# A two-layer decoder: gate weights stationary and tokens moving, a new order around the compressed blocks, transposes of layer 0 behind two more steps, and another split of the last output tile

## The chip, the cores and the metric

The kernel runs on one core of a Trainium2 chip. Its engines work side by side, each through its own queue in order: TensorE (PE in the profile; PEld is its loading of weights), VectorE (DVE), ScalarE (ACT), GpSimd (POOL) and SyncE (SP), which here issues transfers. The metric is the device time of one execution in microseconds (us), the median of several runs. Lower is better.

## The reference

The input is 256 tokens of 1024 numbers. Everything is float32.

```
h  = x + stick_breaking_attention(rms_norm(x)) @ w_o          # 16 heads of 64
h  = h + squared_relu_mlp(rms_norm(h))                         # 1024 -> 4096 -> 1024
kv = rms_norm(h) @ w_kv                                        # shared: compressed, selected, window
     hid = gelu(blocks of 32 tokens, stride 16, + cmp_pos) @ cmp_w1)
     k_cmp, v_cmp = hid @ cmp_w2                               # 15 compressed blocks, 4 groups
q, gate logits = rms_norm(h) @ w_q
gates = sigmoid(gate logits + gate_b)                          # 3 for each of 16 heads
h  = h + (gates * [compressed, selected, window attention]) @ w_o
h  = h + squared_relu_mlp(rms_norm(h))
out = rms_norm(h)
```

Stick-breaking attention takes its weights from a running sum over the keys of log(1 - sigmoid(z)), and so needs, for each pair of heads, Exp, Ln, a scan, a subtraction and one more Exp between the scores z and the product with the values.

## The kernel before, in words

Tokens lie in two tiles of 128 (`t`). A product is made of three matmuls: every float32 operand is split into a rounded part and the rest (`wh` by a cast on ACT, line 125; `wl` by a subtraction on DVE, line 126), and L177, L178 and L179 (`mm3`) multiply high by high, high by low, low by high. L182 (`mm`) is a single matmul, L185 (`tr`) a transpose on PE. Weights come in one stream of transfers on SP into three raw slots, and are split into three slots of `wh` and `wl`; `step()` splits the next half as the program goes on.

*Layer 0.* `proj(n)` makes queries and keys of head pair n with 48 matmuls of 256 columns, six for each of eight k. `inside(n)` inserts the attention of earlier pairs ahead of k = 5 (k = 2 for n = 1): `scores(n-1)` (8 matmuls into z, then the chain of Exp, Ln, scan L507, subtraction L508 and Exp L509), `turn(n-2)` (six transposes, L519, into pa, then copies) and `values(n-3)` (8 matmuls, po). The last pairs are inserted into the out projection at places (i, n, kk).

*Layer 1.* The table `NSA` at the head of the file is the order of its pieces by name. PE is held to that order. A scheduler of the language places the instructions of the other engines, whose queues then run in order. The names that matter here: `kv` projections of keys and values, `gt` and `ga` the transposes and gathers of compressed blocks, `gp` the gates, `cw` the first product of the compressed blocks, `ge` their gelu (copy, Square, Exp, Ln, Exp on ACT, products on DVE), `ch` the transposes of the hidden values (pht), `ck` compressed keys and values (pkc, pvc), `q` a group's half of the query projection (24 matmuls), `qr` its rotation, `S` the scores of a head pair (8 matmuls into z), `M` their softmax weights, `T` the transposes of these (ptp), `V` the values, `o` the out projection. Letters such as 'zzaz' choose between two sets of four PSUM banks, `bank` ('a') and `bank2` ('z'). The function that makes the gates holds the tokens as the stationary operand and moves 96 (high part) or 48 (low part) gate columns: 8 k, two token tiles, two matmuls each.

*The end.* The second MLP accumulates into four banks. Its last products go tile by tile, the last of them in two pieces of 256 columns (`by_t`; the second piece into a bank of its own, accq). `finish` adds each piece to the residual (L268), takes the sum of squares (ACT, L963), the product with the norm's weight (DVE), at the last piece the power on POOL, and scales the tile: ACT columns 0 to 511, DVE 512 to 1023, each followed by a transfer of 256 KB out, on ACT's and on SP's queue.

Of the kernel before, what the change touches and what calls it, by code (L numbers as in the profile page):

```python
# [14 lines left out]
P = 128  # L15
# [21 lines left out]

NSA = (
# [16 lines left out]
def hybrid_kernel(ctx, tc, x, xcols, eye, gcols, gfin, wqk, wv, wo0, wkv, wq, wg, rot, wo1, w1, w2, cw1, cw2, cpos, gate_b, consts, out):  # L55
# [19 lines left out]
    def bank(name, dt=F32):  # L75
        return ps.tile([P, 512], dt, tag="a", name=name, bufs=4)

    def bank2(name):
        return ps.tile([P, 512], F32, tag="z", name=name, bufs=4)
# [101 lines left out]
    def mm(o, a, b, first, last):  # L181
        pe(nc.tensor.matmul(o, a, b, start=first, stop=last, skip_group_check=True))  # L182
# [12 lines left out]
    def tok(xt, k, t):  # L195
        return xt[0][:, k, t * P:(t + 1) * P], xt[1][:, k, t * P:(t + 1) * P]
# [92 lines left out]
    def mlp(layer, gi, xt, mid, ap):  # L289

        wa, wb = i_m[layer]
        acc = [[None, None], [None, None]]
        held = []
        r2 = []

        def second(items, order, hook=None):
            for i, (t, n, q) in enumerate(order):
                if hook is None and i % 2 == 0:
                    step()
                for c, hT, w in items:  # L300
                    for f in range(2):
                        if c == 0 and f == 0:
                            acc[n][t] = bank(f"acc{t}{n}")
                        if q.start and c == items[0][0] and f == 0:

                            acc[n][t] = bank2("accq")
                        o = f * D + n * 512
                        mm3(acc[n][t][:, q], tok(hT, f, t), cut(w, o + q.start, o + q.stop),
                            f == 0 and c == (items[0][0] if q.start else 0), c == NFC - 1 and f == 1)
                if hook is not None:  # L310
                    hook(i, t, n, q)

        whole = slice(0, 512)
        by_n = [(t, n, whole) for n in range(2) for t in range(T)]

        by_t = [(t, n, whole) for t in range(T) for n in range(2)][:-1] + [(1, 1, slice(0, 256)), (1, 1, slice(256, 512))]

        begun = {}

        def begin(c):  # L320

            w = W(wa[c])
            begun[c] = w, [bank2(f"pu{f}") for f in range(2)]
            if c < 2:
                products(c, [(f, k, i) for k in range(NK // 2) for f in range(2) for i in range(2)])

        def products(c, ks, done=None):
            w, pu = begun[c]
            for j, (f, k, i) in enumerate(ks):
                if j % 16 == 0 and (c or j):  # L330
                    step()
                wide(pu[f], cut(w, k * 256 + f * P, k * 256 + (f + 1) * P), xt, k, i, k == 0, k == NK - 1)
                if k == NK - 1 and i:
                    done(f, pu[f])

        def first(c):
            if c not in begun:
                begin(c)
            r = ap.tile([P, 512], F32, name="mr")
            u = ap.tile([P, 512], F32, name="mu")  # L340
            s = ap.tile([P, 512], F32, name="ms")

            def done(f, pu):

                q = slice(f * 256, (f + 1) * 256)
                nc.scalar.copy(r[:, q], pu[:, 256:512])  # L346
                nc.vector.tensor_add(u[:, q], pu[:, 0:256], r[:, q])  # L347

            products(c, [(f, k, i) for f in range(2) for i in range(2) for k in range(NK // 2 if c < 2 else 0, NK)], done)
            nc.vector.scalar_tensor_tensor(s, u, 0.0, u, op0=OP.max, op1=OP.mult)  # L350
            hh = ap.tile([P, 2, T * P], F32R, name="hh", bufs=3)
            hl = ap.tile([P, 2, T * P], F32R, name="hl", bufs=3)
            sv = s.rearrange("p (f q) -> p f q", f=2)
            nc.scalar.copy(hh, sv)  # L354
            nc.vector.tensor_sub(hl, sv, f32(hh))  # L355
            return hh, hl


        begin(0)
        pt = xt_tr(1, bank)  # L360
        begin(1)
        xt_evac(pt, 1, gi, xt)
        for c in range(NFC):
            hT = first(c)
            if c == 0:
                for t in range(T):
                    r = sp.tile([P, 1], F32, name="r2", bufs=4)
                    nc.vector.reciprocal(r, var_of([hres[t]]))
                    r2.append(r)
            if 0 < c < NFC - 1:  # L370
                second([held.pop(0) + (W(wb[c - 1]),)], by_n)
            held.append((c, hT))

        def hook(i, t, n, q):
            res(n, t, acc[n][t], r2[t], q if q.start else whole)
            mid(i, t, n, q)

        second([it + (W(wb[it[0]]),) for it in held], by_t if layer else by_n, hook)

    def layer0(ap):  # L380
# [152 lines left out]


        def inside(n):
            return {2 if n == 1 else 5: [lambda f=f, p=n - d: f(p) for d, f in ((1, scores), (2, turn), (3, values)) if n >= d]}

        for n in range(NP):
            proj(n, inside(n))
        xn = xt_tiles("n")  # L540
        out_proj(oT, i_o0, {(0, 0, 2): [lambda: scores(NP - 1), lambda: values(NP - 3)],
                            (0, 1, 0): [lambda: turn(NP - 2)], (0, 1, 2): [lambda: values(NP - 2)],
                            (1, 0, 0): [lambda: turn(NP - 1)], (1, 0, 1): [lambda: values(NP - 1)],
                            (1, 1, 2): [lambda: xt_evac(xt_tr(0), 0, 1, xn)]})
        return xn
# [1 line left out]
    def nsa(xk, pt0, ap):  # L547
# [63 lines left out]
        M = NG * NC  # L611
        blk = [None, None]
        ph = None

        def gather_tr(c):
            live["g", c] = []
# [52 lines left out]
        gates = ap.tile([P, T, 48], F32, name="gates")  # L669

        def gate_proj():
            pg = bank("pg")
            for k in range(NK):
                for t in range(T):
                    h, lo = tok(xq, k, t)
                    mm(pg[:, t * 96:(t + 1) * 96], h, wgp[:, k].rearrange("p a c -> p (a c)"), k == 0 and t == 0, False)
                    mm(pg[:, t * 96:t * 96 + 48], lo, wgp[:, k, 0, :], False, k == NK - 1)
            g2 = ap.tile([P, T, 96], F32, name="g2", tag="pe", bufs=6)
            for t in range(T):
                nc.scalar.activation(g2[:, t], pg[:, t * 96:(t + 1) * 96], AF.Copy, scale=rstd[t])  # L680
            nc.vector.tensor_add(gates, g2[:, :, 0:48], g2[:, :, 48:96])
            nc.vector.tensor_add(gates, gates, gbs[:, None, :].to_broadcast([P, T, 48]))
            nc.vector.tensor_scalar(gates, gates, -80.0, None, op0=OP.max)
            nc.scalar.activation(gates, gates, AF.Exp, scale=-1.0)
            nc.vector.tensor_scalar(gates, gates, 1.0, None, op0=OP.add)
            nc.vector.reciprocal(gates, gates)

            nc.vector.tensor_tensor(gates[:, :, 0:NH], gates[:, :, 0:NH],
                                    cst[:, C_ANY:C_ANY + T][:, :, None].to_broadcast([P, T, NH]), op=OP.mult)

        live = {}

        qu = big([P, NG, 2, T * P], F32, "qu")
        qr = big([P, NG, 2, T * P], F32, "qr")
# [228 lines left out]
        def tokens_n():  # L923
# [3 lines left out]


        strict[0] = True
        do = {"kv": kv_proj, "xq": tokens_q, "rt": rot_tables, "gt": gather_tr, "ga": gather, "gp": gate_proj, "kr": keys_rope,  # L930
              "cw": cw_proj, "kt": keys_tr, "q": q_proj, "qr": q_rot, "ge": gelu, "ch": cmp_hid, "ck": cmp_kv, "S": scores,
              "M": weights, "T": turn, "V": values, "cp": cmp_probs, "ct": cmp_tr, "o": o_proj, "r": residual, "xn": tokens_n,
              "w": step}
# [25 lines left out]
    def finish(i, t, n, q):  # L959
# [12 lines left out]
            return  # L972
        r = sp.tile([P, 1], F32, name="r", bufs=4)
        nc.gpsimd.tensor_tensor(r, v, npow, op=OP.pow)
        nc.scalar.activation(y[:, 0:512], y[:, 0:512], AF.Copy, scale=r)
        nc.vector.tensor_scalar(y[:, 512:1024], y[:, 512:1024], r, None, op0=OP.mult)
        nc.scalar.dma_start(out[t * P:(t + 1) * P, 0:512], y[:, 0:512])
        nc.sync.dma_start(out[t * P:(t + 1) * P, 512:1024], y[:, 512:1024])

    scoped(mlp, "m1", 1, 3, xn, finish)  # L980

# [93 lines left out]
```

## Time and profile before

| | us |
|---|---|
| median of the runs | 630.44 (629.31, 630.44, 630.53) |
| the profiled execution | 631.12 |
| its span, first to last instruction | 629.3 |
| mean granted TensorE clock | 0.995 |
| PE busy | 617.7 (98%) |
| DVE busy | 418.1 (66%) |
| ACT busy | 344.5 (55%) |

A row of the timeline gives start, length, engine, line, operation, output <- inputs, and in brackets the idle time ahead of it and what ended that. A row of the waits gives the total, the count and the longest. A row of the chain of waits gives start, length to the next step of the chain, engine, tile and line. Matmuls overlap their neighbours, so their spacing is less than their length.

### The profile page before, as it was taken

The numbers are of one execution on the slowest core, as the hardware profiler recorded it, in microseconds if no ns is written. First come the engines' busy times: TensorE is split into PE (matmuls) and PEld (weight loads), VectorE is DVE, ScalarE is ACT, GpSimd is POOL, SyncE is SP. The second block draws the span as 40 slices with busy tenths as digits, with TensorE's granted clock in tenths as the row PEclk, the third lists the DMA queues.
The fourth block names the chain that finished last, engine by engine and source line by source line (L and its number), as shares of the span: only waits on it lengthen the run. The fifth ranks groups of instructions, "written<-read, shape, count | busy, mean of one in ns | idle before, by whom it ended". The sixth has DMA issues, their size and how long they took to land.

```text
span 629.3 us, 9078 instructions
## 1 busy us (share of the span) xinstructions
PE 617.7 (98%) x3569; PEld 518.4 (82%) x3569; DVE 418.1 (66%) x667; ACT 344.5 (55%) x592; POOL 55.4 (9%) x76
## 2 busy tenths in 40 slices
PE   8999999999999999999999989999999999999996
PEld 5899987888888888888888867777888888888885
DVE  5587887766566666656783599863685656666555
ACT  5666666465444445443852597773565544444533
POOL 0100000000000000000322164460000000000000
PEclk9999999999999999999989999999999999999999
DMA  8863333446555455553554731303455554545501
GB/s 290 348 262 135 134 134 117 159 168 227 200 169 203 169 206 191 201 200 135 175 212 189 276 125 70 101 2 134 134 200 202 193 201 154 205 184 200 202 0 68
DMA packets 17755, 108.12 MB, mean 172 GB/s; under 512 B 2352, under 2 KB 3248, under 8 KB 5680
## 3 DMA queue, kind: packets, MB, share of 16 engines
q1 hardware_dynamic: 16416, 105.84, 46.5%
q10 hardware_dynamic: 1296, 1.70, 0.9%
q8 instruction: 28, 0.46, 0.3%
q14 instruction: 15, 0.12, 0.1%
HBM read 106.48 MB, written 1.05 MB: 171 GB/s over the span
## 4 chain that ended last, share of the span: by engine, by line
PE 91%; DVE 3%; ACT 3%; issue 1%; DMA 1%; SPq 0%; POOLq 0%; POOL 0%; DVEq 0%
PE pu L182 28%; PE acc L177 12%; PE acc L178 11%; PE acc L179 11%; PE po L182 3%; PE qk L177 2%; PE qk L179 2%; PE qk L178 2%; PE z L182 2%; PE pk L177 2%; PE pk L179 2%; PE pk L178 2%; PE ptp L185 1%; ACT pe L850 1%; PE ph L182 1%; PE pv L177 1%
## 5 line engine op out<-in xcount | busy, mean ns | idle before, releaser
L126 DVE TENSOR_TENSOR wl<-raw,wh 128x1024 fp32r<-128x1024 f32 (+1 forms) x190 | 226.6, 1228 | 126.3 <-ACT wh L125 125.2
L125 ACT CAST wh<-raw 128x1024 fp32r<-128x1024 f32 (+1 forms) x190 | 189.5, 1041 | 105.4 <-PE acc L179 50.7
L182 PE MATMUL pu<-xn,wh 128*128 128x512 f32 x512 | 132.1, 392 | 0.0
L182 PEld LDWEIGHTS pu<-xn,wh 128*128 128x128 f32 x512 | 93.7, 188 | 18.0
L177 PE MATMUL acc<-wh,hh 128*128 128x512 f32 (+1 forms) x256 | 99.9, 390 | 0.0
L178 PE MATMUL acc<-wl,hh 128*128 128x512 f32 (+1 forms) x256 | 99.7, 389 | 0.0
L179 PE MATMUL acc<-wh,hl 128*128 128x512 f32 (+1 forms) x256 | 98.8, 388 | 0.0
L182 PE MATMUL pu<-xn,wl 128*128 128x256 f32 x512 | 76.5, 282 | 0.0
L182 PEld LDWEIGHTS pu<-xn,wl 128*128 128x128 f32 x512 | 72.1, 190 | 5.1
L179 PEld LDWEIGHTS acc<-wh,hl 128*128 128x128 f32 x256 | 48.1, 188 | 10.7 <-DVE hl L355 0.6
L177 PEld LDWEIGHTS acc<-wh,hh 128*128 128x128 f32 x256 | 48.2, 188 | 10.1 <-ACT hh L354 0.9
L178 PEld LDWEIGHTS acc<-wl,hh 128*128 128x128 f32 x256 | 48.2, 188 | 8.7
L354 ACT CAST hh<-ms 128x512 fp32r<-128x512 f32 x32 | 19.8, 620 | 63.1 <-DVE ms L350 63.1
L346 ACT COPY mr<-pu 128x256 f32<-128x256 f32 x64 | 23.6, 368 | 28.3 <-PE pu L182 28.3
L177 PE MATMUL qk<-xa,wh 128*128 128x256 f32 x128 | 36.9, 288 | 0.0
L179 PE MATMUL qk<-xa,wl 128*128 128x256 f32 x128 | 36.3, 283 | 0.0
L178 PE MATMUL qk<-xa,wh 128*128 128x256 f32 x128 | 36.2, 283 | 0.0
L355 DVE TENSOR_TENSOR hl<-ms,hh 128x512 fp32r<-128x512 f32 x32 | 22.1, 691 | 19.2 <-ACT hh L354 19.2
L864 POOL TENSOR_TENSOR pe<-pe,rs 128x512 f32<-128x512 f32 (+1 forms) x32 | 32.3, 1038 | 25.4 <-DVE rs L859 10.0
L850 ACT ACTIVATE pe<-pe,nm 128x256 f32<-128x256 f32 (+1 forms) x64 | 28.2, 443 | 6.3 <-DVE nm L848 4.6
L347 DVE TENSOR_TENSOR mu<-pu,mr 128x256 f32<-128x256 f32 x64 | 26.6, 418 | 7.5 <-ACT mr L346 7.5
L177 PE MATMUL acc<-wh,oT 128*128 128x512 f32 x64 | 26.3, 411 | 0.0
(184 smaller groups left out, 860.1 us busy)
## 6 DMA issues: line engine op xcount, KB each, us to landing
raw<-in_w SPq DMA_DIRECT2D x64, 1024.0 KB, 4.8
raw<-in_wqk SPq DMA_DIRECT2D x8, 1024.0 KB, 5.0
raw<-in_wo SPq DMA_DIRECT2D x8, 1024.0 KB, 4.8
raw<-in_wkv SPq DMA_DIRECT2D x6, 1024.0 KB, 4.8
raw<-in_wq SPq DMA_DIRECT2D x4, 1024.0 KB, 4.8
wc<-in_cw SPq DMA_DIRECT2D x4, 1024.0 KB, 7.6
raw<-in_wv SPq DMA_DIRECT2D x7, 512.0 KB, 8.5
hres<-in_x SPq DMA_DIRECT2D x2, 512.0 KB, 8.8
```

What stands on the lines that cost most here:

```text
L125: nc.scalar.copy(h[:, r], raws[j][:, r])
L126: nc.vector.tensor_sub(lo[:, r], raws[j][:, r], f32(h[:, r]))
L177: pe(nc.tensor.matmul(o, a[0], b[0], start=first, stop=False, skip_group_check=True))
L178: pe(nc.tensor.matmul(o, a[0], b[1], start=False, stop=False, skip_group_check=True))
L179: pe(nc.tensor.matmul(o, a[1], b[0], start=False, stop=last, skip_group_check=True))
L182: pe(nc.tensor.matmul(o, a, b, start=first, stop=last, skip_group_check=True))
L346: nc.scalar.copy(r[:, q], pu[:, 256:512])
L347: nc.vector.tensor_add(u[:, q], pu[:, 0:256], r[:, q])
L354: nc.scalar.copy(hh, sv)
L355: nc.vector.tensor_sub(hl, sv, f32(hh))
L850: nc.scalar.activation(e, e, AF.Exp, scale=-1.0, bias=nm[:, hd, t, b:b + 1], accum_out=rs[:, hd, t, b:b + 1])
L864: nc.gpsimd.tensor_tensor(sv, sv, rs[:, hd, t, :][:, :, None].to_broadcast([P, 2, n]), op=OP.mult)
```

## The change

Five things change. `turn(n-2)` leaves the common insertion and goes ahead of k = 7; in the out projection three insertions become one at (0, 0, 3). The gates hold the weights (96 or 48 columns) and move all 256 tokens, so 16 matmuls make the transposed gates; ACT copies them out, and a new piece `gq` behind `gt` 1 transposes them back with two transposes, before the same elementwise work. In the table, `q` 1 0 goes behind `cw` 1, `ge` ahead of `q` 1 1, and `ch` and `ck` go ahead of `q` 2 0 and `q` 2 1. The last output tile is cut at 384 of 512 columns instead of 256. In the final scaling ACT has 384 columns and DVE 640, and the transfers are cut there too.

```diff
 NSA = (
-    ('ga', 0), ('gp',), ('kv', 2, 0), ('gt', 1), ('kr', 0), ('kv', 2, 1), ...
-    ... ('qr', 0), ('q', 1, 0), ('kt', 1),
-    ('cw', 1, 0), ('cw', 1, 1), ('q', 1, 1), ('S', 0, 'zzaz'), ('M', 0), ('ge',), ('qr', 1), ('S', 1, 'azzz'), ('M', 1), ('q', 2, 0),
-    ('q', 2, 1), ('ch',), ('w',), ('T', 0, 'zaa'), ('S', 2, 'azaz'), ('ck',), ('q', 3, 0), ('T', 1), ('qr', 2),
+    ('ga', 0), ('gp',), ('kv', 2, 0), ('gt', 1), ('gq',), ('kr', 0), ('kv', 2, 1), ...
+    ... ('qr', 0), ('kt', 1),
+    ('cw', 1, 0), ('cw', 1, 1), ('q', 1, 0), ('ge',), ('q', 1, 1), ('S', 0, 'zzaz'), ('M', 0), ('qr', 1), ('ch',),
+    ('q', 2, 0), ('S', 1), ('M', 1), ('ck',), ('q', 2, 1), ('w',), ('T', 0, 'zaa'), ('S', 2, 'azaz'), ('q', 3, 0),
+    ('T', 1), ('qr', 2), ...
...
-        by_t = [(t, n, whole) for t in range(T) for n in range(2)][:-1] + [(1, 1, slice(0, 256)), (1, 1, slice(256, 512))]
+        by_t = [(t, n, whole) for t in range(T) for n in range(2)][:-1] + [(1, 1, slice(0, 384)), (1, 1, slice(384, 512))]
...
         def inside(n):
-            return {2 if n == 1 else 5: [lambda f=f, p=n - d: f(p) for d, f in ((1, scores), (2, turn), (3, values)) if n >= d]}
+            h = {2 if n == 1 else 5: [lambda f=f, p=n - d: f(p) for d, f in ((1, scores), (3, values)) if n >= d]}
+            if n >= 2:
+                h[7] = [lambda: turn(n - 2)]
+            return h
...
-        out_proj(oT, i_o0, {(0, 0, 2): [lambda: scores(NP - 1), lambda: values(NP - 3)],
-                            (0, 1, 0): [lambda: turn(NP - 2)], (0, 1, 2): [lambda: values(NP - 2)],
+        out_proj(oT, i_o0, {(0, 0, 3): [lambda: scores(NP - 1), lambda: values(NP - 3), lambda: turn(NP - 2)],
+                            (0, 1, 2): [lambda: values(NP - 2)],
...
         def gate_proj():
-            pg = bank("pg")
+            pg = bank2("pg")
             for k in range(NK):
-                for t in range(T):
-                    h, lo = tok(xq, k, t)
-                    mm(pg[:, t * 96:(t + 1) * 96], h, wgp[:, k].rearrange("p a c -> p (a c)"), k == 0 and t == 0, False)
-                    mm(pg[:, t * 96:t * 96 + 48], lo, wgp[:, k, 0, :], False, k == NK - 1)
+                mm(pg[0:96, 0:T * P], wgp[:, k].rearrange("p a c -> p (a c)"), xq[0][:, k, :], k == 0, False)
+                mm(pg[0:48, 0:T * P], wgp[:, k, 0, :], xq[1][:, k, :], False, k == NK - 1)
+            gT = ap.tile([96, T * P], F32, name="gT", tag="pe", bufs=6)
+            nc.scalar.copy(gT, pg[0:96, 0:T * P])
+            live["gT"] = gT
+
+        def gate_turn():
+            pg = bank2("pgt")
+            gT = live.pop("gT")
+            for t in range(T):
+                pe(nc.tensor.transpose(pg[:, t * 96:(t + 1) * 96], gT[:, t * P:(t + 1) * P], ident[0:96, 0:96]))
             g2 = ap.tile([P, T, 96], F32, name="g2", tag="pe", bufs=6)
...
-        nc.scalar.activation(y[:, 0:512], y[:, 0:512], AF.Copy, scale=r)
-        nc.vector.tensor_scalar(y[:, 512:1024], y[:, 512:1024], r, None, op0=OP.mult)
-        nc.scalar.dma_start(out[t * P:(t + 1) * P, 0:512], y[:, 0:512])
-        nc.sync.dma_start(out[t * P:(t + 1) * P, 512:1024], y[:, 512:1024])
+        m = 384
+        nc.scalar.activation(y[:, 0:m], y[:, 0:m], AF.Copy, scale=r)
+        nc.vector.tensor_scalar(y[:, m:D], y[:, m:D], r, None, op0=OP.mult)
+        nc.scalar.dma_start(out[t * P:(t + 1) * P, 0:m], y[:, 0:m])
+        nc.sync.dma_start(out[t * P:(t + 1) * P, m:D], y[:, m:D])
```

On PE, in layer 0, this is one of the insertions inside the projections as the two programs differ (rows of the change with +, of before with -):

```order
 L182 MATMUL z_573<-qkT 128x128
 L182 MATMUL z_574<-qkT 128x128
-L519 MATMUL pa<-ident,sbe 128x128 x6
 L182 MATMUL po<-sbt,v_92 64x256 x2
 L182 MATMUL po<-sbt,v_92 64x128 x2
```
```order
 L178 MATMUL qk<-xa,wh 128x256
 L179 MATMUL qk<-xa,wl 128x256
+L519 MATMUL pa<-ident,sbe 128x128 x6
 L177 MATMUL qk<-xa,wh 128x256
 L178 MATMUL qk<-xa,wh 128x256
```

The six transposes stood between scores and values; they now stand alone among projection matmuls, 12 of these later.

On ACT, around the gelu of layer 1 (hx and hu are its tiles, qu the queries of a group, pe the softmax weights, hidT the turned hidden values), before:

```order
L740 COPY hx<-ph 60x512
L125 CAST wh<-raw 128x1024
L712 ACTIVATE qu<-pq 128x512
L743 ACTIVATE hu<-hx 60x512
L850 ACTIVATE pe,rs<-pe,nm 128x256 x4
L850 ACTIVATE pe,rs<-pe,nm 128x128 x4
L125 CAST wh<-raw 128x1024
L746 ACTIVATE hu<-hu 60x512
L850 ACTIVATE pe,rs<-pe,nm 128x256
L747 ACTIVATE hu<-hu 60x512
L850 ACTIVATE pe,rs<-pe,nm 128x256
L748 ACTIVATE hu<-hu 60x512
```

and in the change:

```order
L749 COPY hx<-ph 60x512
L752 ACTIVATE hu<-hx 60x512
L755 ACTIVATE hu<-hu 60x512
L756 ACTIVATE hu<-hu 60x512
L125 CAST wh<-raw 128x1024
L757 ACTIVATE hu<-hu 60x512
L721 ACTIVATE qu<-pq 128x512
L859 ACTIVATE pe,rs<-pe,nm 128x256 x4
L859 ACTIVATE pe,rs<-pe,nm 128x128 x4
L767 COPY hidT<-pht 128x240
```

The gelu no longer stands among the softmax weights of two head pairs; its last Exp stands behind one weight cast.

On DVE, at the very end (v is the mean of squares so far), before:

```order
L964 TENSOR_TENSOR ys_4138<-hres_72,gf 128x256
L969 SCALAR_TENSOR_TENSOR v<-ssq_4136 128x1
L268 SCALAR_TENSOR_TENSOR hres_72<-accq,r_4235,hres_72 128x256
L971 COPY ssq_4136<-v 128x1
L964 TENSOR_TENSOR ys_4138<-hres_72,gf 128x256
```

and in the change:

```order
L973 TENSOR_TENSOR ys_4127<-hres_72,gf 128x384
L978 SCALAR_TENSOR_TENSOR v<-ssq_4125 128x1
L980 COPY ssq_4125<-v 128x1
L268 SCALAR_TENSOR_TENSOR hres_72<-accq,r_4224,hres_72 128x128
L973 TENSOR_TENSOR ys_4127<-hres_72,gf 128x128
```

The copy of v stands ahead of the last addition where it stood behind it, and the last pieces are half as wide.

More of the change, by code (lines that the diff above doesn't have):

```diff
@@ L613, in nsa @@
         ph = None
+        live = {}
         def gather_tr(c):
@@ L689, in gate_proj @@
                                     cst[:, C_ANY:C_ANY + T][:, :, None].to_broadcast([P, T, NH]), op=OP.mult)
-        live = {}
         qu = big([P, NG, 2, T * P], F32, "qu")
@@ L929, in nsa @@
         strict[0] = True
-        do = {"kv": kv_proj, "xq": tokens_q, "rt": rot_tables, "gt": gather_tr, "ga": gather, "gp": gate_proj, "kr": keys_rope,
+        do = {"kv": kv_proj, "xq": tokens_q, "rt": rot_tables, "gt": gather_tr, "ga": gather, "gp": gate_proj, "gq": gate_turn, "kr": keys_rope,
               "cw": cw_proj, "kt": keys_tr, "q": q_proj, "qr": q_rot, "ge": gelu, "ch": cmp_hid, "ck": cmp_kv, "S": scores,
```

6 rows, old and new, of the table NSA are left out of this document.

## The prediction

> **What bounds the kernel now.** I read the page's totals first, then the waits of TensorE (PE), the chain of waits, and the timeline and windows at the places that the change touches. The totals of the page:
>
> ```profile
> PE 617.7 (98%) x3569; PEld 518.4 (82%) x3569; DVE 418.1 (66%) x667; ACT 344.5 (55%) x592; POOL 55.4 (9%) x76
> ```
>
> PE is busy for 617.7 of 629.3 us. An edit moves the end only by the matmul time it takes out, by an idle stretch of PE that it closes or opens, by the clock it is granted, or in the tail behind the last matmul. PE's larger waits behind its start, by what ended them (total us, times, longest):
>
> ```profile
> PE pht L756 <- DVE hu L749: 1.0, 1, 1.0
> PE pa L519 <- ACT sbe L509: 0.9, 1, 0.9
> PE z L182 <- DVE nm L848: 0.6, 1, 0.6
> PE ptp L185 <- POOL pe L864: 0.3, 1, 0.3
> ```
>
> Those are what an order can win, 2.8 us. None of them ends on a DMA. Sums are made against the profiled execution (631.12 us: span 629.3 and 1.8 around it), which lies 0.7 above the median of the runs, 630.44. Differences are carried over unchanged.
>
> **Layer 0's transposes.** The chain of waits (start, us, engine, tile, line), at the first insertion that holds a turn, at the second and the last of those inside the projections, and in the out projection:
>
> ```profile
> 46.43 0.86 ACT sbe L509
> 47.33 0.88 PE pa L519 x6
> 54.81 0.81 PE pa L519 x6
> 88.40 0.80 PE pa L519 x6
> 99.74 0.66 PE pa L519 x6
> ```
>
> Ahead of 47.33 PE waits 0.9 for the last Exp of the probabilities, which begins at 46.43. The six transposes now come two k steps later, behind 12 matmuls of 256 columns, which start 0.12 apart:
>
> ```profile
> 358.43 0.28 PE L179 MATMUL pq<-xq,wl 128*128 128x256 f32 x1
> 358.55 0.28 PE L177 MATMUL pq<-xq,wh 128*128 128x256 f32 x1
> ```
>
> That is 1.44 us of work from 46.4, where PE stood idle, so it ends near 47.9, and the Exp is over at 47.29: the wait goes, -0.9. What comes late next is the copy of the transposes, which the values read one block on. A block takes 8.4 us (54.81 to 88.40 is four), 1.4 of which the move takes away, so nothing waits. In the other five blocks six transposes cost 0.80 to 0.81 packed between scores and values; where they stand alone among wide matmuls they cost 0.66: 5 x 0.15 = -0.75. In the out projection the same number of matmuls stands in fewer, longer insertions: nothing. Sum -1.65; bounds -0.9 (a border costs the same wherever it stands) and -1.8.
>
> **The gates.** Before, 32 matmuls move 96 or 48 gate columns; after, 16 move 256 tokens. The timeline, and windows of PE (from:to length, busy and count, granted clock, DMA share, GB/s):
>
> ```profile
> 322.79 3.99 PE L182 MATMUL pg<-wgp,xq 128*128 128x96 f32 x32
> 326.61 0.77 PE L177 MATMUL pk<-wh,xk 128*128 128x512 f32 x1
> 329.57 0.40 PE L178 MATMUL pk<-wl,xk 128*128 128x512 f32 x1
> 329.81 0.40 PE L179 MATMUL pk<-wh,xk 128*128 128x512 f32 x1
> 333.46 1.03 PE L185 MATMUL ptc<-ident,kd 128*128 128x128 f32 x8
> ```
> ```profile
> 322.50:325.90 3.40, 3.40 (x32) 1.00 0.97 393
> 325.90:329.30 3.40, 3.40 (x12) 0.50 0.01 5
> ```
>
> For one stretch of 3.4 us right behind the narrow matmuls the clock is halved, though PE's busy time shows no gap; the narrow matmuls are all that sets this place apart. From 322.79 to 329.57 are 6.78 us, the gates and seven matmuls of 512 columns. After: 16 x 0.12 = 1.92 and 7 x 0.24 = 1.68, at full clock: 3.6. That is -3.2, of which seven slowed matmuls make up about (329.57 - 326.61) - 1.68 = 1.3. The two new transposes of the gates go by the last row of the timeline, 8 in 1.03 with the last one's 0.27 of length: 0.11 each, +0.22. Sum -2.95. New on ACT is one copy of 96x256, which two steps of the table cover ahead of the two transposes; uncovered it costs PE 0.37:
>
> ```profile
> L346 ACT COPY mr<-pu 128x256 f32<-128x256 f32 x64 | 23.6, 368 | 28.3 <-PE pu L182 28.3
> ```
> Without the dip before would take 3.1 us to 325.90 and the remaining 0.7 us of the gates at twice the speed, 3.5 in all; the gain is then 3.5 - 1.92 - 0.22 = 1.35, and 1.6 of the 2.95 hangs on the dip.
>
> [...]
>
> Against the change speaks a border between stationary operands of different widths, which alternates now 16 times (96 and 48 columns):
>
> ```profile
> 403.90 0.39 PE L182 MATMUL po<-pcT,vcb 128*64 128x256 f32 x2
> 404.30 0.60 PE L185 MATMUL pct<-ident,ce 128*60 128x128 f32 x4
> 404.73 1.47 PE L185 MATMUL ptp<-ident,pe 128*128 128x128 f32 x12
> ```
>
> From the last pair of po to pct it takes 0.40. From pct (60 columns held) to ptp (128) nothing is lost: four pct go by in 0.43. So a gate matmul takes 0.12 to 0.40, 0 to 4.5 more in all. I take 0.12, since the second border changes only the size, as here, and the first also passes from products to transposes.
>
> **Projections, gelu and compressed blocks.** The rows of before around the other three waits, and a window of all engines (busy of PE, PEld, DVE, ACT, POOL):
>
> ```profile
> 361.14 1.04 ACT L125 CAST wh<-raw 128x1024 fp32r<-128x1024 f32 x1 [2.06 <-PE pq L178]
> 362.31 0.42 DVE L848 CUSTOM_DVE_ANT_0 pe<-z,nmask 128x256 f32<-128x256 f32 x1 [1.09 <-PE z L182]
> 361.15 2.85 PE L182 MATMUL z<-kT,qr 64*128 64x512 f32 x14
> 364.54 0.67 PE L182 MATMUL z<-kT,qr 64*128 64x256 f32 x2 [0.55 <-DVE nm L848]
> 365.16 0.68 DVE L744 SCALAR_TENSOR_TENSOR hu<-hu,hx 60x512 f32<-60x512 f32 x1
> 369.70 0.62 ACT L748 ACTIVATE hu<-hu 60x512 f32<-60x512 f32 x1
> 370.99 1.10 DVE L749 TENSOR_TENSOR hu<-hu,hx 60x512 f32<-60x512 f32 x1
> 360.00:400.00 40.00, 37.66 (x302) 30.56 (x301) 37.51 (x131) 32.41 (x105) 21.71 (x20) 1.00 0.24 84
> ```
>
> Between S 0 and S 1 now lie 24 matmuls (2.9 us), while VectorE (DVE) empties a piece of z in 0.42, so the z wait (0.6) goes. T 0 now follows 24 matmuls more, so POOL's scaling is done: the ptp wait (0.3) goes. After each idle stretch the first matmul also loses its overlap of 0.16 (0.28 long at 0.12 spacing): 0.3 together. More, shorter insertions add about 0.1 of borders: -1.1.
>
> The pht wait (1.0) stays. In the new ACT order the last Exp of the gelu stands behind a weight cast that needs the slot which q(1,1) reads to its end. From that end: cast 1.04, Exp 0.62, what is left of a z piece on DVE, 0 to 0.42, and the product, 0.68 to 1.10: 2.3 to 3.2, and I take 2.6, DVE being in the midst of z. PE has S 0 to do, 8 of 16 z matmuls, some 1.5. The wait is 1.1, as before. Bounds: it goes and 1.0 more is won, if ACT has the Exp done ahead of that cast; the sum is 0, if DVE, 37.5 of 40 us busy here, is what really holds PE back and the waits return under other names. Two transfers of cw 1 stand earlier in SP's queue, ahead of a weight of the out projection; none of PE's waits ends on a DMA, and I cost it at nothing; a transfer that came late would show as a wait of ACT's cast.
>
> **The tail.** Rows behind the last full accumulation:
>
> ```profile
> 620.01 0.28 PE L177 MATMUL acc<-wh,hh 128*128 128x256 f32 x1
> 621.68 0.74 DVE L268 SCALAR_TENSOR_TENSOR hres<-acc,r,hres 128x512 f32<-128x512 f32 x1
> 622.45 0.42 ACT L963 ACTIVATE ys<-hres 128x256 f32<-128x256 f32 x1 [0.66 <-DVE hres L268]
> 623.00 0.16 DVE L969 SCALAR_TENSOR_TENSOR v<-ssq 128x1 f32<-128x1 f32 x1
> 623.08 0.48 DVE L268 SCALAR_TENSOR_TENSOR hres<-accq,r,hres 128x256 f32<-128x256 f32 x1
> L963 ACT ACTIVATE ys<-hres 128x512 f32<-128x512 f32 x3 | 1.9, 635 | 3.9 <-DVE hres L268 3.9
> 624.96 0.72 ACT L975 ACTIVATE ys<-ys,r 128x512 f32<-128x512 f32 x1 [0.85 <-POOL r L974]
> 624.96 0.49 DVE L976 TENSOR_SCALAR ys<-ys,r 128x512 f32<-128x512 f32 x1 [0.66 <-POOL r L974]
> ```
>
> The last tile's first piece is now 384 columns: 12 matmuls at 0.18 (between 0.12 and 0.24) instead of 0.12, so L268 starts 0.7 later, at 622.4. The second addition, at 623.08, does not follow PE's last matmul but stands on DVE behind v, and v behind ACT's sum of squares of the first piece, now 0.1 longer (0.42 for 256 columns, 0.635 for 512). The copy of v now also stands ahead of it. So it starts 0.9 later, near 624.0. The last piece is half as wide: -0.13 on DVE (0.74 against 0.48 for 256 columns), -0.1 on ACT. The scaling starts 0.7 later, and DVE's part is 640 wide, +0.12 (0.49 for 512); ACT's is 384, -0.15. The two output transfers follow them: +0.7. Bounds: -0.3, if the addition takes its place behind PE (only the narrower piece counts), and +1.05.
>
> **Sum.** -1.65 - 2.95 - 1.1 + 0.7 = -5.0: 626.1 for a profiled execution, **625.4** on the median.
>
> **The rivals.** (1) The runs compared hold no dip, or both kernels have one: 1.6 of the gain is not there, 627.0. For it: the runs shown differ by 1.2 among themselves, which is the size of the dip; against it: two of three are at the upper value, with the profiled one 0.7 above. (2) DVE is the bound from 360 to 400 and gives back what the new order wins: 1.1 less gain, 626.5, or 627.3 with the transposes of layer 0 no cheaper. For it: 37.5 of 40; against it: PE has 37.7 there. (3) The tail gains and the pht wait is covered: each is worth 1.0, so 624.4 with one of the two and 623.4 with both. For it: nothing in the order, which puts v and a cast ahead. (4) The other side: the mixed widths make each gate matmul take 0.40, the array stands half idle, and the clock dips here too: 16 x 0.40 = 6.4, seven matmuls at half clock 2.96, transposes 0.22, together 9.6 for 6.78: +2.8 in place of -2.95, with the rest (-2.05) 0.75 above before, 631.2. It decides from 0.35 us between gate matmuls. Against it: the pct border at 0.11. That the order does not do what the table says is out: PE keeps it.
>
> **How the numbers follow.** Forecast 0.52 (its own range 624.6 to 626.3), (1) 0.2, (2) 0.13, (3) 0.1, (4) 0.05. The range 623.9 to 627.7 leaves out (4), the far half of (3) and some of (2). A measurement of this kernel tells 0.2%, 1.26 us, from no change: slower by the upper part of (4) or a cost I do not see, 0.04; within it by the rest of (4) and the far ends of (1) and (2) together, 0.07; faster 0.89.
>
> **What would show it.** Sixteen pg matmuls in about 1.9 us with the granted clock at 1.00 behind them; the pa wait gone from PE's waits and blocks of six at 0.66; z and ptp gone, pht still near 1; the addition of the last piece 0.9 later against the start of the 12 matmuls ahead (3.07 after 620.01 before). It is wrong if pg takes over 5 us, if the clock dips elsewhere, or if new waits on DVE over 1 us stand between S 0 and T 1.

## The result

The changed kernel takes 626.63 us in the median of six runs (626.16 to 627.12), the kernel before 629.88 beside it: a ratio of 0.9949, with an interval of 0.9936 to 0.9962, or 3.25 us less. Forecast were 625.4 in a range of 623.9 to 627.7 and 5.0 us less. The profiled execution went from 631.12 to 626.89, and its span from 629.3 to 625.1.

The traces tell where. The table gives, for the profiled executions, the time between the starts of first matmuls: of layer 0 from qk to the first pu; around the gates from the first ptc to pr; of the attention of layer 1 from pr to the first pu of the second MLP; and from there to the end of the span. "Before, again" is a second profiled execution of the kernel before, taken later. What is left of a span lies ahead of qk, where it differs by up to 1 us from execution to execution, and in the first MLP, where it does not differ.

| kernel | layer 0 | gates | attention of layer 1 | second MLP and tail |
|---|---|---|---|---|
| before | 91.11 | 29.90 | 98.66 | 184.29 |
| before, again | 91.11 | 28.31 | 98.55 | 184.24 |
| changed | 89.31 | 26.78 | 98.76 | 185.05 |
| forecast of the difference | -1.65 | -2.95 (-1.35 without the dip) | -1.1 | +0.7 |
| measured | -1.80 | -3.12 (-1.53) | +0.1 to +0.2 | +0.76 to +0.81 |

Three terms are met within 0.2 us. The attention of layer 1 is the one that is missing.

The chain of waits of the changed kernel at the first and the last turn inside layer 0's projections, and at the first in the out projection:

```profile
47.99 0.66 PE pa L519 x6
89.23 0.66 PE pa L519 x6
96.36 0.81 PE pa L519 x6
```

The first two, and those between, take 0.66, and the wait for the Exp is gone from PE's waits. The turn in the out projection went the other way: it now stands packed behind scores and values and takes 0.81, where it took 0.66. The timeline at the gates, and windows of PE there (from:to length, busy and count, granted clock, DMA share, GB/s):

```profile
320.87 2.04 PE L182 MATMUL pg<-xq,wgp 128*96 128x256 f32 x16
322.74 0.40 PE L177 MATMUL pk<-wh,xk 128*128 128x512 f32 x1
324.36 0.39 PE L178 MATMUL pk<-wl,xk 128*128 128x512 f32 x1
```
```profile
321.03:324.43 3.40, 3.40 (x24) 1.00 0.85 352
324.43:327.83 3.40, 3.40 (x17) 1.00 0.12 14
```

Behind the first of the sixteen matmuls it is 1.87 us to the projection's next one, 0.117 for each, and from the first of them to the eighth pk it is 3.49 us where it was 6.78. The clock stays full. The two widths that alternate cost nothing, which settles the fourth rival.

PE's larger waits now:

```profile
PE pht L765 <- DVE hu L758: 1.3, 1, 1.3
PE po L182 <- ACT pcT L824: 1.3, 1, 1.3
PE pct L185 <- DVE ce L815: 0.3, 1, 0.3
```

z and ptp are gone as forecast and pht stays as forecast. (Of these waits some differ between executions of one kernel: in the second profile of before pht is 1.5 and ptp is not in the list.) But po waits 1.3 for the copy of the turned compressed probabilities, where it was 0.3, and pct waits 0.3, where it did not. What stands ahead of that copy in the changed kernel, on DVE and ACT:

```profile
378.93 0.40 DVE L805 TENSOR_REDUCE cmx<-psc 128x16 f32<-128x240 f32 x1
384.41 1.03 ACT L125 CAST wh<-raw 128x1024 fp32r<-128x1024 f32 x1
385.83 0.57 ACT L824 COPY pcT<-pct 60x512 f32<-60x512 f32 x1
```

and in the kernel before:

```profile
384.46 0.39 DVE L796 TENSOR_REDUCE cmx<-psc 128x16 f32<-128x240 f32 x1
390.28 0.56 ACT L815 COPY pcT<-pct 60x512 f32<-60x512 f32 x1
```

From the softmax's first step to the copy it was 5.82 us and is 6.90; the difference is the one weight cast, 1.03, that now stands ahead of the copy on ACT. From pr to the po that waits for this copy it was 44.54 us and is 45.15, 0.61 more. Most of that comes back later, at a place that the list of waits does not show. The eight matmuls into one later z (the row before, then that of the change) took 2.29 us and take 1.56:

```profile
407.51 2.29 PE L182 MATMUL z<-kT,qr 64*128 64x512 f32 x8
403.01 1.56 PE L182 MATMUL z<-kT,qr 64*128 64x512 f32 x8
```

The z after it takes 0.30 longer, and the attention as a whole ends 0.1 to 0.2 later. The timeline of the tail:

```profile
615.07 0.33 PE L177 MATMUL acc<-wh,hh 128*128 128x384 f32 x1
618.80 0.16 DVE L978 SCALAR_TENSOR_TENSOR v<-ssq 128x1 f32<-128x1 f32 x1
619.07 0.34 DVE L268 SCALAR_TENSOR_TENSOR hres<-accq,r,hres 128x128 f32<-128x128 f32 x1
620.70 0.62 ACT L985 ACTIVATE ys<-ys,r 128x384 f32<-128x384 f32 x1 [0.85 <-POOL r L983]
```

The last addition begins 4.00 after the first matmul of the piece (3.07 before), and the scaling 5.63 (4.95 before). The addition stands behind v, as forecast.

### The profile page after: what moved, and what is told of

Same layout as the page of the kernel before. It is cut to its first block, busy times and chain, and to the rows that moved or that the text cites. A ratio compares the mean times of both kernels' runs of the same rounds, so it can differ in the third digit from the quotient of the medians.

```text
span 625.1 us, 9055 instructions
## 1 busy us (share of the span) xinstructions
PE 613.3 (98%) x3555; PEld 516.1 (83%) x3555; DVE 416.7 (67%) x667; ACT 344.6 (55%) x593; POOL 54.1 (9%) x76
## 4 chain that ended last, share of the span: by engine, by line
PE 90%; DVE 4%; ACT 2%; issue 1%; DMA 1%; SPq 0%; POOLq 0%; POOL 0%; DVEq 0%
PE pu L182 29%; PE acc L177 12%; PE acc L178 11%; PE acc L179 11%; PE po L182 3%; PE qk L177 3%; PE qk L179 2%; PE qk L178 2%; PE z L182 2%; PE pk L177 2%; PE pk L178 2%; PE pk L179 2%; PE ptp L185 1%; ACT pe L859 1%; PE ph L182 1%
## 5 line engine op out<-in xcount | busy, mean ns | idle before, releaser
L126 DVE TENSOR_TENSOR wl<-raw,wh 128x1024 fp32r<-128x1024 f32 (+1 forms) x190 | 225.9, 1224 | 124.1 <-ACT wh L125 116.3
```

The source lines that it names most:

```text
L126: nc.vector.tensor_sub(lo[:, r], raws[j][:, r], f32(h[:, r]))
```

## The experiments

The runs came in three groups of four kernels, each group with its own executions of the kernel before between them. Ratios are to these.

**The kernel before, again.** No edit.

> The kernel before, unchanged, to see how its executions spread. [...]

Measured: 12 executions, median 629.05, and 29 of the same kernel among the others, 629.26 (ratio 1.0001, 0.9986 to 1.0016). The mean granted clock sorts them, all but one (630.05 at 0.997). Of the 41, 28 have a clock of 0.997 or more and a mean of 629.0 us; 10 have 0.994 to 0.996 and a mean of 630.7; 3 have 0.992 and 631.8. In the two later groups it is 13 of 23 and 5 of 11 with the full clock, with means of 628.9 and 629.0, against 630.5 and 630.6 for the others. The profiled execution here was one at full clock (628.78, clock 0.999). Its windows and its timeline at the gates:

```profile
322.20:325.60 3.40, 3.40 (x33) 1.00 0.96 371
325.60:329.00 3.40, 3.40 (x17) 1.00 0.16 29
```
```profile
322.19 3.65 PE L182 MATMUL pg<-wgp,xq 128*128 128x96 f32 x32
325.68 0.49 PE L177 MATMUL pk<-wh,xk 128*128 128x512 f32 x1
```

The same 32 narrow matmuls, and no dip behind them; the stretch of the gates is 1.59 us shorter than in the first profile (28.31 for 29.90). So about two executions in five of the kernel before carry 1.6 us that the others do not, and the profile that the forecast worked from was one of them. One execution of each kind was profiled, so that the 1.6 us stand at the gates in the others too is not shown by this run; the gates alone, below, bear on it.

**Layer 0 alone.** `inside` and the insertions of the out projection as in the change, all else as before.

> The kernel before with only the transposes of layer 0 moved. Prediction as recorded: -1.65 us (0.9 of a wait, 0.15 for each of five blocks). Theory from the changed kernel's trace: -1.7 to -2.0, with all seven blocks of six transposes at 0.66 inside the projections and no pa wait. Rival (a border costs the same wherever it stands): -0.9.

Measured: 627.11, ratio 0.9961 (0.9947 to 0.9975). Executions at full clock: 627.1 against 628.9, so -1.8. In the trace layer 0 is 89.31 us, as in the full change. Six transposes, borders included, take 0.66 among wide matmuls and 0.80 packed between scores and values.

**The gates alone.**

> The kernel before with only the gates turned (16 matmuls with the weights held, the copy, two transposes). Theory: 16 matmuls in 1.9 us and no halved clock behind them in any execution. Against executions of before without the halved clock -1.35 us; against the mean of all of them, a third having it at 1.6 us, -1.9; the clock of all executions at 0.997 or more. Rival (the halved clock has another cause than narrow matmuls): -1.35, and still some executions at a clock of 0.995.

Measured: 627.40, ratio 0.9967 (0.9955 to 0.9978), or -2.1. All eight executions have a clock of 0.997 or more, and their mean is 627.55, 1.4 below those of before at full clock. The gates stretch is 26.77. Both halves of the theory hold in this kernel. Taken over the six kernels with the gates turned and no wait of over 1.5 us in the attention (this one, the changed one in both its groups, and four below), 36 of 40 executions have a clock of 0.997 or more. The other four have 0.996: two of the changed kernel's first six (627.12 and 626.32) and two of the last kernel below. So most of the low clocks go with the narrow matmuls, and not all.

**The gates in halves.** The kernel before with its narrow matmuls in two pieces of four k each; of the edit, the table:

```diff
-    ... ('kv', 1, 0), ('gt', 0), ('kv', 1, 1),
-    ('ga', 0), ('gp',), ...
+    ... ('kv', 1, 0), ('gt', 0), ('gp', 0), ('kv', 1, 1),
+    ('ga', 0), ('gp', 1), ...
```

> The kernel before with its 32 narrow gate matmuls unchanged but made in two groups of 16, six k steps of keys and values between them. [...]

Measured: 629.26, ratio 0.9998 (0.9988 to 1.0009). Ten of 11 executions have the full clock, against 28 of 41 of the kernel before beside them; with one low execution in 11, chance alone gives such a difference, to either side, about one time in four, and against all 75 executions of before (46 at full clock) about one time in eleven. It points to fewer low clocks where the narrow matmuls stand in two pieces (1 of 11 for 13 of 41), and does not settle it.

**The order alone.** The new order of projections, gelu and compressed blocks on the kernel before.

> The kernel before with only the new order of query projections, gelu and compressed blocks. Prediction as recorded: the waits of z and ptp go, 1.1 us faster than before. Theory from the changed kernel's trace: the same waits go, but a weight cast now stands ahead of the copy of the compressed probabilities on ScalarE, the wait of po for pcT grows from 0.3 to 1.3, and the sum is between -0.2 and +0.2 us against before.

Measured: 629.39, ratio 1.0002 (0.9991 to 1.0013). PE's waits around the compressed blocks:

```profile
PE pht L756 <- DVE hu L749: 1.3, 1, 1.3
PE po L182 <- ACT pcT L815: 1.3, 1, 1.3
PE pct L185 <- DVE ce L806: 0.3, 1, 0.3
```

The attention takes 98.75 here as in the full change, for 98.55 to 98.67 in the kernels with the old order. The forecast's -1.1 is wrong, and by this part alone.

**The tail undone.** The changed kernel with its tail as before.

> The changed kernel with its last output tile cut at 256 of 512 columns and scaled half and half, as before. Theory (the wider first piece makes the last addition late): 0.7 us faster than the changed kernel, near 625.9 on the scale of 626.6, and from the first of the twelve matmuls of that piece to the end of the span 9.3 us instead of 10.0. Rival (the new cut gains, because the last piece is shorter, and the loss seen is noise of the transfers): 0.3 us slower than the changed kernel.

Measured: 625.45, ratio 0.9940 (0.9926 to 0.9955), with 184.24 us from the second MLP to the end for 185.05. From the first of the twelve matmuls to the end it is 9.28 and was 10.04, as forecast. The changed kernel by itself took 626.30 in another group (below). Undoing the tail wins 0.8.

**Only the cut undone.** The cut at 256 again, the scaling and the transfers left at 384 and 640.

> The changed kernel with the last tile's accumulation cut at 256 again, but the final scaling and the transfers at 384 and 640. Theory (the loss is the late last addition alone): the 0.7 us are won back as with both undone, 625.5 on the scale of 625.5 for both undone. Rival (the larger transfer at the end costs, 320 KB instead of 256): 0.3 us or more slower than both undone.

Measured: 626.01, ratio 0.9939 (0.9923 to 0.9955); 184.40 us in the trace. So of the 0.81 the cut is 0.65, and the uneven scaling and transfers are left with 0.16, which is little beside the spread of the profiles with the old tail (184.24 to 184.30). By the medians this kernel is 0.56 slower than with both undone, which is the rival's side; but the two were timed in different groups, and of the 0.96 between the two profiled spans 0.80 lie ahead of the first qk, where neither edit stands. What the uneven part costs by itself stays open.

**The changed kernel, again.**

> The changed kernel, unchanged, beside the three below. Theory from the parts (layer 0 -1.8, gates -1.4, order 0.1, tail +0.7, against executions of before at full clock): 2.4 us under those of before, near 626.5 where these are at 629.0, with the clock at 0.997 or more in nearly all executions. Rival (the parts help each other): 3.2 or more under them.

Measured: 626.30, ratio 0.9947 (0.9929 to 0.9965). All five executions have the full clock, with a mean of 626.47 against 629.03 for those of before at full clock: -2.6, by the parts -1.80 - 1.53 + 0.15 + 0.78 = -2.4. Against the median of all executions of before, six of eleven with the low clock, it is -3.9. The parts add up; what moves the ratio is how many executions of before have the low clock.

**The hidden values later.** The changed kernel with `ch` behind `q` 2 0.

> The changed kernel with the transposes of the hidden values behind the 24 matmuls of the next query projection's first half instead of ahead of them. Theory (PE waits 1.3 there for the gelu's last product, and 24 matmuls, 2.9 us, cover it): the pht wait goes, -1.2 us against the changed kernel. Rival (VectorE is the bound from here to the first values, so the time comes back at the next wait on it): -0.4 or less, with a longer wait for z, pct or pcT.

Measured: 631.46, ratio 1.0029 (1.0019 to 1.0040), 5 us slower than the changed kernel. The wait at pht goes and a larger one comes. From PE's waits, POOL's timeline and PE's windows:

```profile
PE pvc L182 <- POOL hv L769: 4.4, 1, 4.4
```
```profile
362.99 4.66 POOL L873 TENSOR_TENSOR pe<-pe,rs 128x512 f32<-128x512 f32 x4 [3.14 <-ACT wh L125]
367.60 0.58 POOL L769 COPY hv<-hidT 128x480 f32<-128x480 f32 x1
```
```profile
364.40:367.80 3.40, 0.00 (x0) 0.93 0.68 236
367.80:371.20 3.40, 2.96 (x21) 0.50 0.20 77
371.20:374.60 3.40, 3.40 (x19) 0.56 0.01 2
```

In the changed kernel POOL makes the copy of the hidden values at 362.62 and the scaling of the softmax weights behind it, at 363.68. Here the copy's input is ready at 363.16, when the scaling has begun, and the copy stands behind all 4.7 us of it. PE is idle for 4.4 us, and the clock is then near half for 6.8 us. All twelve executions have a clock of 0.992 or less. Neither theory named this queue.

**The keys later.** The changed kernel with `ck` behind `q` 2 1. On ACT the cast then stands behind the copy pcT.

> The changed kernel with the compressed keys and values made one half projection later; in ScalarE's order this puts a weight cast behind the copy of the turned compressed probabilities instead of ahead of it. Theory (that cast, 1.03 us, is what made the wait of po for pcT grow from 0.3 to 1.3): the wait is 0.3 again, -1.0 us against the changed kernel. Rival (the copy is late since VectorE's softmax of the compressed blocks is late): the wait stays over 0.8, no gain over 0.2 us.

Measured: 631.83, ratio 1.0047 (1.0030 to 1.0063). ACT and PE at pcT, the wait that follows, and PE's windows behind it:

```profile
384.28 0.57 ACT L824 COPY pcT<-pct 60x512 f32<-60x512 f32 x1
384.75 1.99 ACT L125 CAST wh<-raw 128x1024 fp32r<-128x1024 f32 x2
384.90 0.65 PE L182 MATMUL po<-pcT,vcb 128*64 128x256 f32 x4
```
```profile
PE ptp L185 <- DVE nm L857: 2.7, 1, 2.7
```
```profile
388.40:391.80 3.40, 1.12 (x10) 1.00 0.00 0
391.80:395.20 3.40, 2.97 (x16) 0.61 0.00 0
395.20:398.60 3.40, 3.40 (x19) 0.50 0.81 270
```

With the casts behind the copy, 5.83 us pass from the softmax's first step to the copy, as before (5.82), and po does not wait at all: the cast is what made that wait grow. Two steps on, PE waits 2.7 for the next softmax on DVE, and the clock falls again. That wait comes from POOL's queue. On DVE the second half of the rotation (L730) now stands ahead of the maxima of that softmax, and it needs POOL's half (L727), which stands behind 4.6 us of scaling. DVE is idle for 2.3 us:

```profile
389.08 1.26 POOL L727 TENSOR_TENSOR qr<-qu,cs 128x512 f32<-128x512 f32 x1
390.38 0.69 DVE L730 TENSOR_TENSOR qr<-qr,qx 128x512 f32<-128x512 f32 x1 [2.30 <-POOL qr L727]
```

In the changed kernel this step stands behind the maxima (the row L730 at 391.16, they from 388.94), and DVE does not wait. So the 1.0 us at the copy was won, and was lost with more to a row that moved on another engine. An order with the cast behind the copy and L730 behind the maxima was not tried.

**The hidden values inside the projection.** The changed kernel with the tail undone and the transposes behind 12 matmuls of `q` 2 0. No other engine's order changes.

```diff
+                if (g, half, k) == (2, 0, 2):
+                    cmp_hid()
```

> The changed kernel with the tail as before, and the transposes of the hidden values behind the first 12 matmuls of the next query projection instead of ahead of it; no other engine's order changes. Theory (12 matmuls, 1.4 us, cover the pht wait of 1.3, but GpSimd's copy of the hidden values is then ready when it was, so PE waits for it instead): the pht wait is under 0.1, a wait of pkc or pvc of 0.6 to 0.9 appears, -0.5 us against the kernel with only the tail undone. Rival (VectorE holds PE back over the whole stretch): the waits at pcT, pct and z grow by what pht loses, no gain.

Measured: 625.91, ratio 0.9937 (0.9922 to 0.9953), not faster than the tail undone alone (625.45, in another group). The attention takes 98.73, with the tail undone alone 98.76. PE's waits:

```profile
PE po L182 <- ACT pcT L826: 1.3, 1, 1.3
PE z L182 <- DVE rs L870: 0.3, 1, 0.3
PE pct L185 <- DVE ce L817: 0.3, 1, 0.3
PE pvc L182 <- POOL hv L771: 0.2, 1, 0.2
PE pq L177 <- ACT pT L892: 0.2, 1, 0.2
```

The pht wait, 1.3, is gone and nothing is won: new waits of 0.2 to 0.3 stand on DVE, POOL and ACT, and pcT comes when it came. The waits at pcT and pct did not grow, as the rival had said they would, but its outcome, no gain, is what came; the windows under the next kernel show why.

**The keys inside as well.** `ck` behind 6 matmuls of `q` 2 1, which takes the evacuation of the compressed values behind a weight subtraction on DVE.

```diff
+                if (g, k) == (2, 5):
+                    cmp_kv()
```

> As the one before, and the compressed keys and values inside the next half projection, behind 6 matmuls. Theory (the 0.7 us of these matmuls cover the copy too): neither pht nor pkc nor pvc waits over 0.1, -1.0 us against the kernel with only the tail undone, near 624.5. Rival (VectorE holds PE back): the softmax scores wait longer for z, or po for pcT, and the gain is under 0.3.

Measured: 625.46, ratio 0.9936 (0.9919 to 0.9954). The attention takes 98.31, 0.45 less than the changed kernel.

```profile
PE z L182 <- DVE vcb L792: 1.1, 1, 1.1
PE po L182 <- ACT pcT L828: 1.1, 1, 1.1
PE ptp L185 <- DVE kcb L785: 0.6, 1, 0.6
```

Neither pht nor pvc is in the list, and 2.8 us of other waits are. Windows of all engines (busy of PE, PEld, DVE, ACT, POOL), from the gelu's last product on DVE to the last of DVE's maxima ahead of the copy pcT, in the changed kernel, with the hidden values inside, and here:

```profile
358.22:383.63 25.41, 24.36 (x190) 20.67 (x190) 24.96 (x93) 20.43 (x72) 15.47 (x15) 1.00 0.25 89
358.04:383.43 25.39, 24.24 (x187) 20.08 (x186) 24.94 (x93) 20.42 (x72) 15.44 (x15) 1.00 0.26 89
357.48:382.44 24.96, 23.24 (x187) 19.89 (x186) 24.43 (x93) 20.45 (x72) 14.48 (x15) 1.00 0.24 89
```

DVE is busy for all but 0.5 us of each. With the pht wait gone it needs the same time, 25.39 for 25.41, and the attention is the same within 0.03. Here it needs 0.45 less, and the attention is 0.45 shorter. Of that 0.46 lie in the four weight subtractions (L126), which take 5.08 here and 5.54 in the changed kernel; one of them takes 1.21 for 1.99, and the traces do not settle why. So in this stretch DVE sets the pace, in one profiled execution of each kernel, and a wait of PE that an order closes gives nothing unless DVE gets through sooner. Of the six executions four are at full clock (625.3 in the mean) and two at 0.996 (627.0); why, with the gates turned, the traces do not show. This kernel and the one with only the tail undone beat both kernels of the case, at about 625.5, and their times cannot be told apart.

## Why the prediction was right or wrong

**Layer 0: right.** The wait of 0.9 and five borders of 0.15 were forecast, -1.65. Layer 0 alone gave -1.80, in the trace and in the times. Two things that the sum left out nearly cancel: the first turn, which took 0.88 behind its wait, takes 0.66 now, and the turn in the out projection, put at nothing, takes 0.81 for 0.66. The rest, about 0.1, is not traced.

**The gates: right in size, and in mechanism as far as tested.** 3.6 us from pg to the eighth pk were forecast and 3.49 came, with no cost of alternating widths. The two values, with and without the dip, were 0.17 and 0.18 short of the measured ones.

**The dip: rival (1) is half of the truth.** The forecast carried the profiled execution's dip over unchanged to the median of the runs ("Differences are carried over unchanged"). The second profile of before shows the same matmuls without a dip, and the clock of 75 executions is lowered in 29 of them. So, by the two profiles, the gates are worth 1.5 against an execution without the dip and 3.1 against one with it, and the median moves with the share. That the narrow matmuls bring the dip is borne out by the gates alone, none low in eight; why one execution has it and the next has not is not shown. What the traces show is one stretch of 3.4 us at 0.50, in one of the two profiled executions of before and not in the other (1.00 there).

**The attention of layer 1: wrong, by 1.2 to 1.3 us.** The step that failed is the sum "-1.1", made from the waits that go, with the rest held still. The z and ptp waits went. But the order on ACT put a weight cast, 1.03, ahead of the copy pcT, which made a wait of 1.3 from one of 0.3; pct waited 0.3; and pht 1.3 instead of the 1.1 forecast. The forecast follows ACT's order to the gelu's last Exp and names the cast there, and does not follow it to pcT. Beneath it lies rival (2), given 0.13: DVE is the bound "and gives back what the new order wins". The last two experiments bear it out: the time of the attention followed the time that DVE needs for the stretch, within 0.03, and not the wait that was closed. DVE is not behind all of it. The cast on ACT comes behind DVE's softmax, and in the two kernels that lost 5 us POOL's queue held the next result. None of the signs that were to show the forecast wrong caught this: the new wait over 1 us ends on ACT, and behind T 1.

**The tail: right.** +0.7 was forecast, +0.8 came; the addition begins 0.93 later, 0.9 was forecast. The runs split it into 0.65 for the cut and 0.16 for the uneven scaling and transfers, the latter from one trace and not firm.

**The number.** For a profiled execution 626.1 was forecast and 626.89 came, 0.8 more: the attention's 1.2 is missing, and 0.15 of layer 0, 0.17 of the gates and 0.1 ahead of qk and in the first MLP, where no edit stands, came on top. For the median it was 625.4 against 626.63, 1.2 more, since the profiled execution of before, with its dip, lay 0.7 above its median and that of the change 0.26. The median of before moves with the mix of executions: 629.88 with three more runs, and 629.26 with 29 others. 626.63 is in the stated range but outside 624.6 to 626.3, which the forecast gave as its own; it lies between rival (2), 626.5, and rival (1), 627.0, and parts of both came true. The range held because it had been drawn around them, not because the sum was right: 3.25 us were gained for 5.0 forecast.

## What to carry to other kernels

Where PE is held by a chain on other engines, a wait that a new order closes is only won if the engine that ends the next wait is also ahead (with the pht wait of 1.3 us closed the attention took 98.73 us for 98.76); follow each engine's order to the point where the next result is read, not to the wait that goes. Where one of those engines is busy all through the stretch, as DVE was for 24.96 of 25.41 us, count its work first. Before a difference of two profiles is priced, look at the granted clock of several executions: a stretch at half clock may be in one and not in the next (here 3.4 us at 0.50 in one profile of the kernel before, none in the other). A wider piece ahead of the last one delays the last addition if that stands in its engine's queue behind a step that needs the wider piece's sum of squares (here by 0.93 us, from 3.07 to 4.00 behind the piece's first matmul).

## What the runs showed of the hardware

In one of two profiles of the kernel before PE's clock fell behind narrow matmuls while PE showed no gap (3.40 of 3.40 us busy, then 3.4 us at 0.50), and a lower clock shows in 29 of 75 executions of the same program, in 26 of them at about 1.6 us. What the other three, at 0.992 and 2.8 us, have besides is not known. The clock also fell behind an idle stretch of 2.7 us: in the kernel with the keys later the window with that wait was at full clock and the two after it at 0.61 and 0.50. With 4.4 us idle it was 0.50 and 0.56 over 6.8 us. Both are read from one profiled execution each, but every timed execution of the two kernels had a low mean clock: 0.991 or 0.992 with the hidden values later, 0.989 to 0.994 with the keys later (630.51 to 633.95 us). So a wait of a few microseconds cost more than its length here: the attention grew by 5.5 us in both kernels, while the waits listed in it grew by 3.7 us in the one (2.9 to 6.6) and by 2.0 in the other (2.9 to 4.9).
